# A hybrid encoder layer: a later rank for the residual, the second norm and the input factors of chunks 2 and 3

## The chip, the cores and the metric

One core of a Trainium2 chip runs the whole layer in one launch. The metric is device time in microseconds (us), lower is better. The kernel before was timed three times: 2137.07 us in the median, 2134.32 to 2137.93.

## The reference

The layer is a mixer (an S5 state space, a Fourier mixer and windowed attention side by side), an output projection with a residual, and a gated feed-forward network with a width-3 convolution. What matters here is the seam between the two:

```python
        y = jnp.concatenate([y_ssm.astype(x.dtype), y_fft.astype(x.dtype), y_att.astype(x.dtype)], axis=-1) @ w_out[l]
        x = x + gt_m * rms_norm(y, g_post_mix[l])

        h = rms_norm(x, g_pre_ffn[l]) * (1.0 + sc_f) + sh_f
        up = dwconv3(h @ w_up[l], conv_w[l], conv_b[l])
        gate, val = jnp.split(up, 2, axis=-1)
        y = (jax.nn.gelu(gate) * val) @ w_down[l]
        x = x + gt_f * rms_norm(y, g_post_ffn[l])
```

D_MODEL is 1024, SEQ 2048, D_FF 2816, all in float32. x is (1, 2048, 1024).

## The kernel before

Everything is held transposed: channels on the 128 partitions, positions along the free axis. The 2048 positions are cut into four chunks of 512 (c = 0 to 3). Float32 products are made from float16 halves: `mm3` issues three float16 matmuls (high by high, low by high, high by low) for one product.

**The seam.** `proj` (L1412) multiplies each chunk with the output weights, eight row blocks m = 0 to 7, 24 matmuls each. `proj_evac` copies a block out of its bank and adds its squares to a running sum. Then `post` (L1474) does, per chunk: the first norm, the residual (a multiply and an add per quarter of the channels, and a store of the result), the squares of it, the second norm, and the scale and shift for the feed-forward network. Each norm goes through `rnorm` (L344): one matmul with a matrix of ones sums the squares over the partitions, ACT takes a reciprocal root and squares it, and two DVE instructions refine it. The matmul writes a bank of the kind "m", of which there is one (`PTAGS`, L205), so a norm's matmul waits until the norm before it has been read out.

**The input factors.** `hcomb(p)` (L1562) turns the normalised chunks 2p and 2p+1 into seven sums and differences, each split into float16 halves. These feed a scheme of seven products for a 2 by 2 block product (`PLACE`). `hcomb(0)` serves positions 0 to 1023, `hcomb(1)` positions 1024 to 2047.

**The up-projection.** `ffn` (L1652) runs over p = 0, 1 and, in each, over 22 pairs of gate and value columns. A pair has seven products of 12 matmuls, in the order 1, 5, 6, 2, 7, 3, 4. Products 1, 6, 7 and 4 run up in the same bank (the pair's first), so each waits for the read of the one before: product 6 for an ACT copy of product 1, product 7 for an ACT copy of product 6, and product 4 for `up_add`, a DVE instruction that reads the bank after product 7. Product 5 opens a second bank that product 3 goes on in, product 2 has a third. `up_act` then does the convolution (four DVE instructions of 1023 elements, two on ACT), the gelu on ACT and the product with the value half. `wcomb` (L1545) makes the weight factors of a later pair, on DVE and ACT too; at most `W_LEAD` = 3 pairs ahead.

**What sets the order.** The program is recorded by coroutines. `Sched.run` picks the step that can start first by its own cost estimates, gives it a planned start st, and stamps the instructions with a rank (L191):

```python
            self.tc.cur_priority = 1000000 + int(PK * (st - p[4]))
```

PK is 100, p[4] is the third argument of `spawn` (`ahead`). A list scheduler then orders the instructions: on each engine the lowest rank first among those that its own estimates call ready. The result is one fixed sequence per engine (PE, DVE, ACT, POOL, and SP for the DMA issues). On the chip each engine takes its sequence from the top, and an instruction whose input is late holds those behind it.

Below, pair 0 to pair 6 are the first seven pairs of p = 0; their first banks are ps_5498, ps_7871, ps_8027, ps_8183, ps_8355, ps_8516 and ps_8662 in the rows of the order.

Of the kernel before, what the change touches and what calls it, by code (L numbers as in the profile page):

```python
# [43 lines left out]
S5_MUL = "V"  # L44
S5_ADD = "V"
G_M1 = 0
POST_B = 0.0
S5_B = 0.0
ATT_B = 0.0
X_AHEAD = (4, 4)  # L50
# [11 lines left out]
P_POST = 0  # L62
# [140 lines left out]
class Builder:  # L203
# [1208 lines left out]
    def proj(self):  # L1412
        self.x1d = self.dt([P, 8, T], F32)
        self.h2d = self.dt([7, 2, P, 2048], F16)
        for p in range(2):
            self.sc.spawn(self.hcomb(p), 0)
        q = [Fut() for _ in range(32)]
        lead = Sem(3)
        self.sc.spawn(self.wo_stream(q, lead))
        tail = Sem(TAIL)  # L1420
        for c in range(4):
            sl = slice(c * 512, (c + 1) * 512)
            tl = yield ("acq", tail, 1)
            yield ("w", self.f_gm)
            for f in self.f_ya[4 * c:4 * c + 4]:
                ta = yield ("w", f)
            yc = [self.u([2, 2, 512], F16) for _ in range(3)]
            fk = [Fut() for _ in range(5)]
            for k, f in enumerate(self.f_yssm + self.f_yfft):
                self.sc.spawn(self.yc_load(k, tl, f, yc[k // 2][:, k % 2], sl, fk[k]), 1)  # L1430
            ys = [self.u([2, 512]) for _ in range(4)]
            acc = self.u([2, 512])
            fs = [Fut() for _ in range(8)]
            for m in range(8):
                tw = yield ("w", q[8 * c + m])
                w = q[8 * c + m].val
                tb = yield ("acq", self.bank["z"], 1)
                ps = self.ps("z")
                t = max(tb, tw, tl, self.f_gm.t)
                for i, k in enumerate((5, 6, 7, 3, 4, 0, 1, 2)):  # L1440
                    if k < 5:
                        tk = yield ("w", fk[k])
                        r = yc[k // 2][:, k % 2, HI], yc[k // 2][:, k % 2, LO]
                    else:
                        tk = ta
                        r = self.yatt[c][HI][:, k - 5], self.yatt[c][LO][:, k - 5]
                    t = yield from self.mm3(max(t, tk), ps, (w[:, HI, k], w[:, LO, k]), r, i == 0, i == 7)
                lead.give(t)
                if 8 * c + m == self.ATT1:
                    self.f_pj.set(t)  # L1450
                if m == 7:
                    self.f_pc[c].set(t)
                self.sc.spawn(self.proj_evac(t, ps, ys[m // 2][:, m % 2], acc, m, fs))
            self.sc.spawn(self.post(c, fs, ys, acc, tail), P_POST if c else 0, 0.0 if c else POST_B)

    def yc_load(self, k, t, f, dst, sl, done):
        t1 = yield ("w", f)
# [652 lines left out]
```

## Time and profile before

| | |
|---|---|
| median of 3 runs (lowest, highest) | 2137.07 us (2134.32, 2137.93) |
| profiled execution, its own time | 2141.4 us |
| its span, first to last instruction | 2139.6 us |
| mean granted TensorE clock | 0.962 |
| PE busy | 1963.9 us, 92% of the span |
| DVE busy | 1559.8 us, 73% |
| ACT busy | 991.0 us, 46% |

Busy shares are means over stages with different limits. The mixer takes the first 840 us or so; chunks 2 and 3 pass the seam between about 860 and 1015 us, while the first pairs of the up-projection run; from there on the up-projection and the down-projection fill the rest. Times within the span are counted from its first instruction. L316 is the line of every matmul, L270 of every ACT instruction, L275 and L289 of DVE's two-input and three-input instructions, so the rows are told apart by shape: `u` is a work tile, `ps` a bank, `c` a constant.

### The profile page before, as it was taken

How to read it: one execution, taken by the hardware profiler on the slowest of the kernel's cores; microseconds unless marked ns; L12 is line 12 of the kernel's file. 1: busy time of each engine (PE TensorE's matmuls, PEld its weight loads, DVE VectorE, ACT ScalarE, POOL GpSimd, SP SyncE). 2: the span in 40 equal slices, each digit the busy share in tenths (PEclk: the TensorE clock that was granted, in tenths of full speed). 3: DMA queues.
4: the chain of work that ended last, by engine and by line, in shares of the span. 5: the costliest groups of instructions: out<-in, count | busy, mean ns of one | idle time of the engine just before them, and what ended most of it. 6: DMA issues, size and time to landing. Idle time of an engine off the chain costs nothing.

```text
span 2139.6 us, 26850 instructions
## 1 busy us (share of the span) xinstructions
PE 1963.9 (92%) x9796; PEld 967.3 (45%) x9796; DVE 1559.8 (73%) x2305; ACT 991.0 (46%) x1666; POOL 244.6 (11%) x310
## 2 busy tenths in 40 slices
PE   6788888789988889997999999999999999999997
PEld 1336764444543444443444444444444444434445
DVE  8998898869677767899988875666565763547356
ACT  3643333355566576665555543444444433322221
POOL 1566554002000000000000000000000000011002
PEclk9989999899999989998999999999999999999998
DMA  9362145673746333346655566656565494548533
GB/s 368 105 209 61 56 127 162 217 247 137 256 144 220 126 125 133 136 179 249 223 197 187 188 216 260 230 189 226 201 217 201 158 334 157 162 134 300 177 100 113
DMA packets 206663, 397.27 MB, mean 186 GB/s; under 512 B 19521, under 2 KB 111938, under 8 KB 206530
## 3 DMA queue, kind: packets, MB, share of 16 engines
q1 hardware_dynamic: 206530, 395.55, 53.7%
q8 instruction: 77, 1.26, 0.2%
q14 instruction: 56, 0.46, 0.1%
HBM read 258.93 MB, written 134.98 MB: 184 GB/s over the span
## 4 chain that ended last, share of the span: by engine, by line
PE 49%; DVE 8%; ACT 2%; issue 1%; DMA 1%; POOL 0%; SPq 0%; POOLq 0%; DVEq 0%; ACTq 0%
PE ps L316 49%; DVE u L289 4%; DVE u L275 3%; ACT u L270 2%; DMA u<-d 0%; DMA u<-w_up 0%; DMA d<-u 0%; ACT L270 0%; POOL u L275 0%; SPq L265 0%; POOLq L2095 0%; DVE u L282 0%; ACT c L270 0%; DVEq L289 0%; DVEq L275 0%
## 5 line engine op out<-in xcount | busy, mean ns | idle before, releaser
L316 PE MATMUL ps<-u,u 128*128 128x512 f16 (+5 forms) x9030 | 1879.2, 368 | 90.7 <-DVE u L289 40.5
L316 PEld LDWEIGHTS <-u 128*128 128x128 f16 (+1 forms) x9058 | 846.8, 99 | 1035.4 <-issue 157.6
L275 DVE TENSOR_TENSOR u<-u,u 128x512 f32<-128x512 f32 (+10 forms) x584 | 506.6, 900 | 105.9 <-ACT u L270 92.4
L270 ACT ACTIVATE u<-u 128x1024 f16<-128x1024 f32 (+7 forms) x485 | 406.0, 869 | 360.9 <-DVE u L275 150.3
L270 ACT ACTIVATE u<-ps 128x512 f32<-128x512 f32 (+8 forms) x497 | 268.7, 555 | 410.4 <-PE ps L316 377.5
L289 DVE SCALAR_TENSOR_TENSOR u<-u,c,u 128x1023 f32<-128x1023 f32 (+5 forms) x248 | 291.3, 1197 | 61.2 <-ACT u L270 53.9
L289 DVE SCALAR_TENSOR_TENSOR u<-ps,u 128x512 f32<-128x512 f32 (+4 forms) x231 | 152.3, 666 | 229.2 <-PE ps L316 199.2
L289 DVE SCALAR_TENSOR_TENSOR u<-u,u 128x1024 f16<-128x1024 f32 (+6 forms) x225 | 240.6, 1093 | 61.4 <-ACT u L270 58.1
L275 POOL TENSOR_TENSOR u<-u,u 128x288 f32<-128x288 f32 (+9 forms) x169 | 187.4, 1123 | 609.3 <-DVE u L289 462.4
L270 ACT ACTIVATE u<-u,c 128x1023 f32<-128x1023 f32 (+3 forms) x106 | 123.5, 1166 | 142.5 <-DVE u L289 122.7
L305 POOL MEMSET u<- 128x1 f32 x88 | 8.6, 98 | 1118.0 <-DVE u L289 415.8
L270 ACT ACTIVATE u<-u,st 128x384 f32<-128x384 f32 (+3 forms) x192 | 107.5, 592 | 30.8 <-DVE st L282 17.3
L316 PEld LDWEIGHTS ps<-u,u 128*128 128x128 f32 (+1 forms) x532 | 91.1, 180 | 39.9 <-DVE u L275 16.8
L316 PE MATMUL ps<-u,c 128*128 128x512 f32 (+4 forms) x142 | 61.8, 551 | 43.5 <-DVE u L300 18.5
L316 PE MATMUL ps<-c,u 128*128 128x128 f16 (+1 forms) x568 | 59.6, 229 | 23.9 <-ACT u L270 18.5
L270 ACT ACTIVATE c<-u 128x2 f32<-128x2 f32 (+1 forms) x88 | 17.8, 202 | 132.3 <-DVE u L289 132.2
L275 DVE TENSOR_TENSOR u<-u 128x512 f32<-128x512 f32 (+8 forms) x136 | 67.8, 502 | 12.4 <-ACT u L270 11.6
L300 DVE TENSOR_TENSOR_SCAN u<-u,u 128x512 f32<-128x512 f32 (+1 forms) x60 | 68.6, 1152 | 0.5
L1330 DVE CUSTOM_DVE_ANT_0 u<-ps,u 128x384 f32<-128x384 f32 (+1 forms) x96 | 48.1, 536 | 23.8 <-PE ps L316 23.7
L289 DVE SCALAR_TENSOR_TENSOR u<-u,st,u 128x384 f16<-128x384 f32 (+1 forms) x96 | 54.6, 603 | 12.2 <-ACT u L270 12.0
L270 ACT ACTIVATE u<-u,c,c 128x512 f32<-128x512 f32 (+1 forms) x64 | 48.4, 804 | 22.3 <-DVE u L275 6.2
L316 PEld LDWEIGHTS ps<-u,c 128*128 128x128 f32 (+1 forms) x142 | 23.9, 190 | 72.6 <-issue 46.6
(52 smaller groups left out, 370.9 us busy)
## 6 DMA issues: line engine op xcount, KB each, us to landing
u<-d SPq DMA_DIRECT2D x226, 512.0 KB
d<-u SPq DMA_DIRECT2D x158, 512.0 KB
d<-u SPq DMA_DIRECT2D x111, 256.0 KB
u<-w_ada SPq DMA_DIRECT2D x48, 512.0 KB
u<-w_up SPq DMA_DIRECT2D x44, 512.0 KB
u<-d SPq DMA_DIRECT2D x66, 256.0 KB
u<-x SPq DMA_DIRECT2D x32, 512.0 KB
u<-d SPq DMA_DIRECT2D x24, 511.0 KB
```

The costliest lines, as they stand in the source:

```text
L270: self.S.activation(out, in_, func, **kw)
L275: (self.V if eng == "V" else self.G).tensor_tensor(out, a, b, op)
L289: self.V.scalar_tensor_tensor(out, a, s, b, op0, op1)
L300: self.V.tensor_tensor_scan(out, d0, d1, 0.0, ALU.mult, ALU.add)
L305: (self.V if eng == "V" else self.G).memset(out, v)
L316: self.PE.matmul(o, a, b, start=st, stop=sp, skip_group_check=chain)
L1330: V.tensor_tensor_reduce(out=s_, in0=o, in1=self.bias[h // 2][:, h % 2, bo:bo + nk * 128], op0=ALU.add, op1=ALU.max, scale=1.0, scalar=-3e ...
```

## The change

The constant `POST_B` becomes a tuple by chunk, and `hcomb` gets an argument. For chunks 2 and 3 and for `hcomb(1)`, `ahead` is -150, which adds 15000 to the rank of every instruction that these coroutines issue: a place 150 us later by the planner's clock. The plan itself, the instructions, the tiles and the banks stay the same.

```diff
-POST_B = 0.0
+LATER = (0.0, 0.0, -150.0, -150.0)
...
         for p in range(2):
-            self.sc.spawn(self.hcomb(p), 0)
+            self.sc.spawn(self.hcomb(p), 0, -150.0 * p)
...
-            self.sc.spawn(self.post(c, fs, ys, acc, tail), P_POST if c else 0, 0.0 if c else POST_B)
+            self.sc.spawn(self.post(c, fs, ys, acc, tail), P_POST if c else 0, LATER[c])
```

The sequences of PE, DVE, ACT and SP change between about 858 and 1080 us of the trace of before; POOL's stays. Three places matter below.

**PE, at the matmul of the second norm of chunk 2** (`ps_7758<-u_7373,c_67`, with `c_67` the matrix of ones; `ps_7752` is the last block of the projection of chunk 3, `ps_7813` the first norm of chunk 3, `ps_8100` product 2 of pair 2, `ps_7871` the first bank of pair 1). Before:

```order
L316 LDWEIGHTS u_7684
L316 MATMUL ps_7752<-u_7423,u_7684 128x512
L316 MATMUL ps_7758<-u_7373,c_67 128x512
L316 LDWEIGHTS u_7684
L316 MATMUL ps_7752<-u_7421,u_7684 128x512
```

After:

```order
L316 LDWEIGHTS u_5625
L316 MATMUL ps_8100<-u_7531,u_5625 128x512
L316 MATMUL ps_7758<-u_7373,c_67 128x512
L316 MATMUL ps_7813<-u_7428,c_67 128x512
L316 LDWEIGHTS u_5493
L316 MATMUL ps_7871<-u_7501,u_5493 128x512
```

It stood within the last projection block. Now 119 more matmuls stand ahead of it: the other 9 of that block, 38 of pair 0 (the rest of products 2 and 7, and products 3 and 4), and products 1, 5 and 2 of pair 1 and of pair 2, 36 each. The first norm of chunk 3 follows at once, in the same bank.

**DVE, at the reader of that norm** (`u_7757<-ps_7758`; `ps_7662`, `ps_5498` and `ps_7606` are pair 0's products 2, 7 and 3, `u_6650` to `u_6653` are chunk 2's four quarters, `u_7881` is pair 0's convolution, `ps_7939` pair 1's product 2). Before:

```order
L275 TENSOR_TENSOR u_7373<-u_7373 128x512
L275 TENSOR_TENSOR u_7428<-u_7428 128x512
L289 SCALAR_TENSOR_TENSOR u_7757<-ps_7758,u_7757 128x512
L289 SCALAR_TENSOR_TENSOR u_7757<-u_7757 128x512
L275 TENSOR_TENSOR u_6650<-u_6650,u_7757 128x1024
L275 TENSOR_TENSOR u_7428<-u_7428 128x512
L289 SCALAR_TENSOR_TENSOR u_5496<-ps_7662,u_5496 128x512
L275 TENSOR_TENSOR u_6651<-u_6651,u_7757 128x1024
L289 SCALAR_TENSOR_TENSOR u_5497<-ps_5498,u_5497 128x512
```

After:

```order
L275 TENSOR_TENSOR u_7428<-u_7428 128x512
L289 SCALAR_TENSOR_TENSOR u_5496<-ps_7662,u_5496 128x512
L289 SCALAR_TENSOR_TENSOR u_5497<-ps_5498,u_5497 128x512
L289 SCALAR_TENSOR_TENSOR u_5496<-ps_7606,u_5496 128x512
L289 SCALAR_TENSOR_TENSOR u_7757<-ps_7758,u_7757 128x512
L289 SCALAR_TENSOR_TENSOR u_7757<-u_7757 128x512
L275 TENSOR_TENSOR u_6650<-u_6650,u_7757 128x1024
L275 TENSOR_TENSOR u_6651<-u_6651,u_7757 128x1024
L275 TENSOR_TENSOR u_6652<-u_6652,u_7757 128x1024
L275 TENSOR_TENSOR u_6653<-u_6653,u_7757 128x1024
L289 SCALAR_TENSOR_TENSOR u_7881<-u_5496,c_1115,u_7881 128x1023
L289 SCALAR_TENSOR_TENSOR u_7869<-ps_7939,u_7869 128x512
```

The reader moved back by four places only: the last sum of squares of chunk 3 and pair 0's three reads now stand ahead of it. All the rest of DVE's work, pair 0's convolution first, stands behind it in both.

**DVE, at the reads of pair 3** (`u_8182<-ps_8183` is the `up_add` that product 4 waits for; `u_8212`, `u_8213`, `u_8222`, `u_8286` and `u_8327` belong to `hcomb(1)`). Before:

```order
L275 TENSOR_TENSOR u_7424<-u_7426,u_7424 128x1024
L275 TENSOR_TENSOR u_8327<-u_8213,u_8326 128x1024
L275 TENSOR_TENSOR u_7425<-u_7427,u_7425 128x1024
L275 TENSOR_TENSOR u_8327<-u_8214,u_8326 128x1024
L289 SCALAR_TENSOR_TENSOR u_8181<-ps_8262,u_8181 128x512
L289 SCALAR_TENSOR_TENSOR u_8182<-ps_8183,u_8182 128x512
```

After:

```order
L289 SCALAR_TENSOR_TENSOR u_8193<-u_8193,u_8194 128x1023
L275 TENSOR_TENSOR u_8184<-u_8184,u_8186 128x512
L289 SCALAR_TENSOR_TENSOR u_8181<-ps_8262,u_8181 128x512
L275 TENSOR_TENSOR u_8222<-u_6651,u_8221 128x1024
L289 SCALAR_TENSOR_TENSOR u_8182<-ps_8183,u_8182 128x512
L275 TENSOR_TENSOR u_8213<-u_7426,u_8211 128x1024
```

The reads come ahead of much of `hcomb(1)`: ten fewer instructions stand ahead of this `up_add`. From the read `u_8661<-ps_8662` of pair 6 (its `up_add` before product 4) on, and already some 30 rows ahead of it, DVE has the same rows behind it in both sequences.

## The prediction

> **What bounds the kernel now.** I read the slices first, then windows over the places where the order changes, then the waits and the chain in them. The slices have 53.5 us each; number 17 covers about 856 to 909, number 20 about 1016 to 1070.
>
> ```profile
> PE   6788888789988889997999999999999999999997
> DVE  8998898869677767899988875666565763547356
> PEclk9989999899999989998999999999999999999998
> ```
>
> PE is full from slice 20 to the end, DVE around slices 18 to 20. The windows say it finer: per row the length, then busy time (and instructions) of each engine, and the granted clock.
>
> ```profile
> 892.00:1005.00 113.00, 98.05 (x431) 42.98 (x430) 108.70 (x116) 73.36 (x101) 1.08 (x11) 0.94 0.49 188
> 1005.00:1068.00 63.00, 60.59 (x280) 27.08 (x278) 59.28 (x66) 37.65 (x56) 0.79 (x8) 1.00 0.64 233
> 1068.00:1200.00 132.00, 132.00 (x613) 59.86 (x612) 107.85 (x116) 72.71 (x104) 1.47 (x15) 1.00 0.53 194
> 1200.00:1700.00 500.00, 500.00 (x2319) 226.68 (x2317) 324.53 (x340) 221.08 (x337) 5.01 (x51) 1.00 0.60 209
> ```
>
> Columns three and four are PE's weight loads and DVE. From 892 to 1068 DVE is busy for 167.98 of 176 us and PE for 158.64: DVE carries the work. From 1068 PE works 132.00 of 132 and DVE has 24 us to spare. So up to 1068 the end moves with DVE's sequence. Behind it PE has no gap in which lateness could run off. What PE lost before 1068:
>
> ```profile
> PE ps L316 <- DVE u L289: 15.1, 5, 10.7
> PE ps L316 <- ACT u L270: 2.1, 5, 0.7
> DVE u L289 <- ACT u L270: 10.3, 7, 3.5
> DVE u L289 <- DMA d<-u: 1.5, 1, 1.5
> ```
>
> These are waits between 860 and 1070: total, times, longest. PE waited 17.2 us, 10.7 of it once, on an `up_add`. The chain of waits shows what that one stood behind, and that nothing stops PE later:
>
> ```profile
> 966.00 2.96 DVE u L275 x3
> 968.96 4.01 DVE u L289 x4
> 972.97 4.54 DVE u L275 x4
> 977.51 1.21 DVE u L289 x2
> 978.77 5.29 PE ps L316 x12
> ...
> 1067.76 432.26 PE ps L316 x2002
> ```
>
> DVE worked without a break through `hcomb(1)`, then read the bank, then PE went on.
>
> **Part one: the `up_add` of pair 3 comes earlier.** Ten instructions fewer stand ahead of it, so the wait of 10.70 us should shrink or go. The rows that follow are PE's alone: start, length up to the next wait, instructions, and the wait ahead of them.
>
> ```profile
> 978.77 21.27 PE L316 MATMUL ps<-u,u 128*128 128x512 f16 x84 [10.70 <-DVE u L289]
> 1001.88 10.10 PE L316 MATMUL ps<-u,u 128*128 128x512 f16 x46 [1.84 <-DVE u L289]
> 1035.52 31.04 PE L316 MATMUL ps<-u,u 128*128 128x512 f16 x142 [0.82 <-DVE u L289]
> 1067.76 7.50 PE L316 MATMUL ps<-u,u 128*128 128x512 f16 x34 [1.21 <-DVE u L289]
> ```
>
> But work that DVE does later isn't done away with. The last two waits stand where DVE's sequence meets PE's again, after all that was put off: if DVE gets there no sooner, PE doesn't, and the gain is only PE's waits in another place. So I go by the time at which DVE gets there.
>
> **Part two: the matmul of chunk 2's second norm comes later on PE.** This decides the sum.
>
> ```profile
> 889.43 1.02 PE L316 MATMUL ps<-u,c 128*128 128x512 f32 x2
> ...
> 891.78 0.69 DVE L289 SCALAR_TENSOR_TENSOR u<-ps,u 128x512 f32<-128x512 f32 x1 [3.49 <-ACT u L270]
> ...
> 1034.78 1.28 DVE L289 SCALAR_TENSOR_TENSOR u<-ps,u 128x512 f32<-128x512 f32 x2
> ```
>
> Before, the matmul starts at 889.43, two ACT instructions follow, and DVE reads the bank at 891.78: 2.35 us later. After, 119 more matmuls stand ahead of it on PE. One takes 132.00/613 = 0.2153 us at the full clock, so they take 25.6 us and the matmul starts at 889.43 + 25.6 = 915.05. Their operands, the factors of positions 0 to 1023 and the first weights, were all written by 868.5 in the trace of before, so I add no wait; any wait would make it later still.
>
> DVE's reader moved back by only four places. Two reads in a row (the last row) take 1.28 us with 0.69 for the second, so a place costs 0.60 and the four 2.4 us. The last of the four reads product 3 of pair 0, which is done 35 of the 119 matmuls on, at 889.43 + 7.5 = 897; so DVE's turn comes at about 898. The bank is ready at 915.05 + 2.35 = 917.4. For some 19 us **DVE has nothing it may do**, with a full sequence behind the reader, in the stage that DVE carries: the rest of chunk 2's norm, pair 0's convolution, every read that PE waits for. PE meanwhile runs ahead until its banks are full and then waits for these reads.
>
> From there DVE's remaining work decides when it meets PE:
>
> ```profile
> 891.70:1035.50 143.80, 127.73 (x567) 56.14 (x565) 138.95 (x149) 91.94 (x129) 1.48 (x15) 0.95 0.54 202
> ```
>
> From that reader to the `up_add` of pair 6, DVE was busy for 138.95 us. After, the same rows are left but the four, 138.95 − 2.4 = 136.5. Without one gap DVE is through at 917.4 + 136.5 = 1053.9, where before PE went on at 1035.52: 18.4 later. By then PE has done 19 matmuls that stood behind this place before, 19 × 0.2153 = 4.1 us, so the end is late by 14.3. The wait of 1.21 at 1067.76 falls away, as PE is no longer ahead of DVE there: **+13.1 us is the low end**.
>
> To it come DVE's gaps. Before, it had 143.80 − 138.95 = 4.85 us of them in this stretch, nearly all waits for ACT (10.3 us from 860 on in the row above, some of it before 891.7). After, ACT starts from the same late norm, and the order of its work for chunk 3's norm, the scale and the bank copies gives the same sort of waits; stepping through the sequences by the trace's durations I get about 4.5. Ends: none (+13.1) and twice as many (+22.1); I take 4.5, as nearest to the row. **13.1 + 4.5 = +17.6 us.**
>
> **What I cost at nothing.** The stores of the residual and the factors of chunks 2 and 3 move behind loads and stores of weights on SP's queue. The weights then go out no later than before against their users, and the stored factors are needed for p = 1 only, hundreds of us on. The only wait on a transfer in the rows above is 1.5 us for a store: ends −1.5 and +1.5, I take 0. Were the cover gone and a weight load late, PE would stop for it in that stage, where it waits for DVE anyway. POOL's sequence stays and it has 1 us of work in 113. ACT is busy for 73.36 of 113: its moved instructions cost through DVE's gaps alone, counted already. The first norm of chunk 3 shares the bank and now follows at once, so PE should stop there about 2 us until DVE has read; PE has slack there.
>
> **PE's clock.** After the wait of 10.70 us, twelve matmuls take 5.29 us in the chain; twelve at 0.2153 are 2.6, so such a restart costs 2.7, and the granted clock is 0.94 from 892 to 1005. The hand timetable that gave the 4.5 has two long stops of PE after the change (about 6 us near 920, about 12 near 971), for the one of before. If they are hidden, since DVE is what comes last, they cost nothing; if the matmuls are on DVE's way, up to 2 × 2.7 = 5.4 more. The Trainium skill ("TensorE: Matmul & The Clock Gate", in "What's actually happening") has PE at half clock after an idle window of about 3.4 us, until it has been busy for one. The trace agrees: half speed for some 5 us after 10.70, none after 1.84. By that rule both stops are followed by a slow start, which speaks against this change, and the sum would be +23.0 instead of +17.6 if neither were hidden.
>
> **The rivals.**
>
> *The slow restarts reach DVE.* Each late product is read by DVE, so a slow one can open a gap there. For it: 10.70 us of idling did halve the speed. Against it: DVE is behind PE by up to a pair's reads there, with other work between. 17.6 + 5.4 = +23.0, 2160.1.
>
> *Faster: DVE doesn't run dry.* If the norm's matmul is ready before DVE's turn, only the savings stay: 10.70 + 1.84 + 0.82 + 1.21 of waits and the 2.7 of the restart, 17.3 us at most, 2119.8. It turns at one place: whether DVE has work until the bank is ready. For it: at the point in question DVE is the fuller engine. Against it: the order has the reader four rows, 2.4 us, later and the matmul 25.6 us later.
>
> *No change.* Lateness runs off before 1068, since PE had 17.2 us of waits there which the later norm may just fill. Against it: DVE's gaps from 891.7 to 1035.5 were 4.85 us in all, and lateness of DVE can run off only there. 2137.
>
> **How the numbers follow.** The profiled execution took 2141.4 us by its own time, with 2139.6 from first to last instruction; the median of the runs is 2137.07, 4.3 lower. The sum is a difference inside the trace: about 2159.0 for a profile, and I put it on the median: 2137.07 + 17.6 = **2154.7**. Chances: the forecast 0.74, the slow restarts 0.12, faster 0.08, no change 0.06. A measurement can tell about 0.2%, 4.3 us, from no change: slower by more than that 0.86, within 0.06, faster 0.08. The low end of the sum is 2150.2; the runs before are spread over 3.6 us, so the range starts 3 lower, at 2147. Above it takes in the twofold gaps (+22.1) and the slow restarts (+23.0), 2160, and ends 2 higher, at 2162. The two cases of the other signs, 0.14, stay outside.
>
> **What would show it.** Right: in the changed profile DVE idles for 15 to 20 us up to about 917, at a read of a bank (L289, released by ACT or PE); the norm's matmul stands near 915; PE's 10.70 wait is gone but has waits of the same sum between 916 and 985; PE is unbroken from about 1060 to 1085 on, everything behind it 15 to 20 us later. Wrong: DVE without a gap at 900 to 915 (then the faster rival holds), or PE with waits beyond 1100 that before doesn't have (then something else is late, weights first), or DVE's busy share from 917 to 1054 far below 0.97 (then ACT's place is mis-sized).

## The result and the profile after

The changed kernel takes 2160.38 us in the median of four runs (2158.64 to 2160.71), beside 2135.86 for the kernel before: 24.5 us more, a ratio of 1.0108 with a 95% interval of 1.0095 to 1.0122, or 20.3 to 26.1 us. Timed a second time beside other kernels it took 2158.92 against 2137.41: 21.5 us more, ratio 1.0095 (1.0081 to 1.0109). The profiled execution has a span of 2158.9 us and its own time is 2160.71.

The slices (54 us each here) show where it went. Slice 17 begins at about 864 us.

```profile
PE   6788888789988799977999999999999999999997
DVE  8998898869677667499998884656565664547356
PEclk9999998899999899988999999999999999999998
```

DVE has a 4 in slice 17 where it had an 8, and PE a 7 in slice 18 where it had a 9. The windows of the changed kernel, with the same columns as before (length, then PE, weight loads, DVE, ACT, POOL, clock, DMA):

```profile
892.00:1005.00 113.00, 88.17 (x367) 37.41 (x365) 84.21 (x89) 60.82 (x84) 0.59 (x6) 0.88 0.34 126
1005.00:1068.00 63.00, 56.42 (x255) 24.63 (x254) 61.26 (x66) 37.95 (x54) 0.98 (x10) 1.00 0.73 271
1068.00:1200.00 132.00, 130.52 (x604) 58.99 (x603) 112.33 (x124) 72.52 (x108) 1.38 (x14) 1.00 0.56 206
1200.00:1700.00 500.00, 500.00 (x2319) 226.68 (x2317) 326.83 (x342) 223.21 (x338) 5.30 (x54) 1.00 0.60 211
```

DVE is busy for 84.21 us of the first 113, and was for 108.70. Most of the loss arises in one smaller window. The kernel before:

```profile
898.00:917.00 19.00, 18.32 (x85) 8.22 (x84) 18.96 (x22) 16.00 (x22) 0.20 (x2) 1.00 0.24 91
```

The changed one:

```profile
898.00:917.00 19.00, 18.23 (x83) 8.03 (x81) 0.00 (x0) 1.50 (x4) 0.00 (x0) 1.00 0.00 1
```

In the same 19 us PE does as much as before. DVE does nothing at all, and ACT, POOL and the DMA next to nothing. The timeline of the changed kernel (start, length, engine, instruction, and in brackets the wait ahead of it) names what they wait for:

```profile
899.87 0.60 ACT L270 ACTIVATE u<-ps 128x512 f32<-128x512 f32 x1 [1.66 <-PE ps L316]
...
915.21 1.02 PE L316 MATMUL ps<-u,c 128*128 128x512 f32 x2
916.27 0.60 ACT L270 ACTIVATE u<-ps 128x512 f32<-128x512 f32 x1 [15.80 <-PE ps L316]
...
917.55 0.69 DVE L289 SCALAR_TENSOR_TENSOR u<-ps,u 128x512 f32<-128x512 f32 x1 [19.58 <-ACT u L270]
...
918.30 1.12 PE L316 MATMUL ps<-u,c 128*128 128x512 f32 x2 [2.07 <-DVE u L289]
```

The norm's matmul starts at 915.21 on PE, behind the products of pairs 0 to 2. ACT stands at the root of its result for 15.80 us, DVE at the read of its bank for 19.58. What PE then waits for, PE's rows alone:

```profile
925.86 13.06 PE L316 MATMUL ps<-u,u 128*128 128x512 f16 x48 [6.43 <-ACT u L270]
...
983.42 0.61 PE L316 MATMUL ps<-u,u 128*128 128x512 f16 x1 [10.25 <-ACT u L270]
984.87 20.14 PE L316 MATMUL ps<-u,u 128*128 128x512 f16 x83 [0.84 <-DVE u L289]
...
1059.54 22.68 PE L316 MATMUL ps<-u,u 128*128 128x512 f16 x103 [0.39 <-DVE u L289]
1082.97 40.18 PE L316 MATMUL ps<-u,u 128*128 128x512 f16 x185 [0.76 <-ACT u L270]
1123.88 601.04 PE L316 MATMUL ps<-u,u 128*128 128x512 f16 x2784 [0.72 <-DVE u L289]
1729.21 0.94 PE L316 MATMUL ps<-u,u 128*128 128x512 f16 x3 [4.30 <-ACT u L270]
```

The row at 1059.54 is product 4 of pair 6 (1035.52 before), the one at 1729.21 is the wait that stood at 1708.70 before. There PE is 20.5 us late, and nothing behind it has another order.

### The profile page after: what moved, and what is told of

Same layout as the page of the kernel before. It is cut to its first block, busy times and chain, and to the rows that moved or that the text cites. A ratio compares the mean times of both kernels' runs of the same rounds, so it can differ in the third digit from the quotient of the medians.

```text
span 2158.9 us, 26856 instructions
## 1 busy us (share of the span) xinstructions
PE 1969.2 (91%) x9796; PEld 968.6 (45%) x9796; DVE 1560.2 (72%) x2305; ACT 989.9 (46%) x1666; POOL 240.6 (11%) x310
## 4 chain that ended last, share of the span: by engine, by line
PE 51%; DVE 6%; ACT 2%; issue 2%; DMA 1%; POOL 0%; SPq 0%; POOLq 0%; DVEq 0%; ACTq 0%
PE ps L316 51%; DVE u L289 4%; ACT u L270 2%; DVE u L275 2%; DMA u<-d 0%; DMA u<-w_up 0%; POOL u L275 0%; ACT L270 0%; SPq L265 0%; POOLq L2095 0%; ACT c L270 0%; DVEq L289 0%; DVEq L275 0%; ACTq L270 0%
## 5 line engine op out<-in xcount | busy, mean ns | idle before, releaser
L270 ACT ACTIVATE c<-u 128x2 f32<-128x2 f32 (+1 forms) x88 | 17.9, 203 | 136.5 <-DVE u L289 136.3
```

The costliest lines, as they stand in the source:

```text
L270: self.S.activation(out, in_, func, **kw)
```

## The experiments

Two theories stood against each other. The first: the matmul of a norm goes back on PE much further than its reader goes back on DVE, and DVE and ACT, which take their instructions in order, run dry. The second: the mass of the put-off work (residual, scale and shift, input factors) is what comes too late. Each run was timed beside the kernel before; differences are of medians, in brackets by the 95% interval of the ratio.

### Half of the change: the input factors, or the chunks

```diff
-LATER = (0.0, 0.0, -150.0, -150.0)
+LATER = (0.0, 0.0, 0.0, 0.0)
```

> Only the input factors of positions 1024 to 2047 get the later rank; both chunks' residual and norms keep theirs. The norm's matmul of chunk 2 and its reader stand where they stood before, the read of pair 3 stands 11 places earlier on DVE, the one of pair 6 at its old place. Theory (the late norm's matmul leaves DVE without work): no idle DVE near 900 to 917, and DVE's place at pair 6 unchanged, so 0 less what PE has done ahead, 3 to 5 us faster than before. Rival (the late input factors and the stops they bring to PE are the loss): 5 to 15 us slower than before. Second rival (PE's waits by themselves are what counts): 13 to 17 us faster, as the 10.70 wait and its slow restart go.

2131.04 against 2136.55: 5.5 us faster (3.2 to 7.9), ratio 0.9974.

```diff
-            self.sc.spawn(self.hcomb(p), 0, -150.0 * p)
+            self.sc.spawn(self.hcomb(p), 0)
```

> Residual and second norm of chunks 2 and 3 late, input factors not. The norm's matmul stands 119 matmuls later, its reader 4 places later, and from the read of pair 3 on DVE's order is that of before. Theory: all of the loss is here, DVE idle about 19 us up to 917, no credit for matmuls done ahead at pair 6: 20 to 24 us slower than before. Rival (late input factors are the loss): within 5 us of before.

2161.77 against 2136.55: 25.2 us slower (22.2 to 28.6), ratio 1.0119, a little above the 20 to 24 us that were expected. DVE is idle for 19.59 us up to 916.70. The loss lies in the chunks' half; the input factors' half is a gain, also a little above its 3 to 5 us. The second theory falls here already, as far as it speaks of the input factors.

### The norm apart from the rest

For these, a coroutine can change its rank on the way (three lines in `_advance`, so line numbers are 3 higher: L319 for matmuls, L292, L278, L273). First everything behind the second norm late, and the norms early (`LATER` and the rank of `hcomb` as in the change):

```diff
+            if r[0] == "rank":
+                p[4], val = r[1], None
+                continue
...
-            self.sc.spawn(self.post(c, fs, ys, acc, tail), P_POST if c else 0, LATER[c])
+            self.sc.spawn(self.post(c, fs, ys, acc, tail), P_POST if c else 0, 0.0)
...
         tr = yield from self.rnorm(sqs, 512, rt[:, 0], rt[:, 1], slack)
         fq = []
+        yield ("rank", LATER[c])
```

> As the change, but chunks 2 and 3 take the later rank only behind the second norm (the products with its result, scale and shift, and the input factors). The matmul of chunk 2's second norm and its reader stand where they stood before. Theory: no idle DVE near 900 to 917; 3 to 5 us faster than before, so 23 to 29 us faster than the change. Rival (work put off behind the norm is the loss): 10 to 24 us slower than before.

2130.26 against 2136.55: 6.3 us faster (3.4 to 8.8), ratio 0.9971, a little above the 3 to 5 us expected, and some 29 us faster than the change. Then the opposite, against the kernel before and with the same three lines in `_advance`: everything at its old rank, and chunk 2's second norm alone late:

```diff
-POST_B = 0.0
+LATER = (0.0, 0.0, -150.0, 0.0)
...
-            self.sc.spawn(self.post(c, fs, ys, acc, tail), P_POST if c else 0, 0.0 if c else POST_B)
+            self.sc.spawn(self.post(c, fs, ys, acc, tail), P_POST if c else 0, 0.0)
...
+        yield ("rank", LATER[c])
         tr = yield from self.rnorm(sqs, 512, rt[:, 0], rt[:, 1], slack)
+        yield ("rank", 0.0)
```

> The order of before, but the second norm of chunk 2 alone (one matmul, two ACT and two DVE instructions) has the later rank; all else keeps its own. Its matmul stands 119 matmuls later, its reader 4 places later. Theory: these five instructions bring the whole loss, 20 to 24 us slower than before, DVE idle about 19 us up to 917. Rival (the mass of the put-off work is the loss): within 5 us of before.

2159.56 against 2136.55: 23.0 us slower (19.9 to 27.3), ratio 1.0111. In its timeline, DVE's row first and then PE's:

```profile
913.48 0.69 DVE L292 SCALAR_TENSOR_TENSOR u<-ps,u 128x512 f32<-128x512 f32 x1 [19.59 <-ACT u L273]
```

```profile
911.13 1.02 PE L319 MATMUL ps<-u,c 128*128 128x512 f32 x2
...
1087.91 636.65 PE L319 MATMUL ps<-u,u 128*128 128x512 f16 x2949 [1.20 <-DVE u L292]
1728.86 1.44 PE L319 MATMUL ps<-u,u 128*128 128x512 f16 x3 [4.29 <-ACT u L273]
```

One norm, five instructions, brings the whole loss, with the same idle time as in the change. The rest of what the change puts off costs nothing; in the version before this one it brings 6 us. Beside the late norm it brings something too: from the norm's matmul, which stands behind the same 119 others in both, to the wait near 1709 it is 1728.86 - 911.13 = 817.7 us here and 1729.21 - 915.21 = 814.0 in the change. These 3.7 us are about the 4.1 us of matmuls done ahead that the prediction counted; between the medians (23.0 us slower here, 24.5 and 21.5 for the change) they are lost in the spread. Windows of the version with the norms early, and two of PE's rows:

```profile
892.00:1005.00 113.00, 103.92 (x470) 45.80 (x468) 112.02 (x118) 78.61 (x107) 1.09 (x11) 1.00 0.53 196
1005.00:1068.00 63.00, 61.23 (x281) 27.18 (x279) 58.14 (x65) 36.91 (x55) 0.89 (x9) 1.00 0.63 233
```

```profile
1052.31 40.18 PE L319 MATMUL ps<-u,u 128*128 128x512 f16 x185 [0.75 <-ACT u L273]
1093.20 601.04 PE L319 MATMUL ps<-u,u 128*128 128x512 f16 x2784 [0.72 <-DVE u L292]
```

DVE fills 112.02 of 113 us (108.70 before) and PE does 39 matmuls more (470 against 431). PE's longest wait up to 1100 is 2.25 us and the clock stays at 1.00. So a wait of 10.70 us and a slow restart of 2.7 are gone, and the end moves by 6.3: part comes back as short waits (PE waits 11.2 us in all between 860 and 1100, where it waited 17.2), since DVE has the same work to do.

### The distance, and another norm

The change with -20 in place of -150, which puts the norm's matmul 71 places later instead of 119:

```diff
-LATER = (0.0, 0.0, -150.0, -150.0)
+LATER = (0.0, 0.0, -20.0, -20.0)
...
-        t = yield from self.ts(t, a, x, -150.0, 89.0, ALU.max, ALU.min)
+        t = yield from self.ts(t, a, x, -20.0, 89.0, ALU.max, ALU.min)
...
-            self.sc.spawn(self.hcomb(p), 0, -150.0 * p)
+            self.sc.spawn(self.hcomb(p), 0, -20.0 * p)
```

The line in the middle isn't part of the idea: the edit also reached a -150 that is the lower bound of a clamp in an exponential (`exp48`). It changes a number that one instruction takes, not the order or the shapes, and the reading below rests on a wait at the seam itself.

> The change with -20 in place of -150. The matmul of chunk 2's second norm stands 71 matmuls later than before instead of 119, its reader 4 places later as in the change; the reads of pairs 3 and 6 stand where the change has them. Theory (loss goes with the matmuls ahead of the norm's): bank ready 48 x 0.2153 = 10.3 us earlier than in the change, DVE idle about 9 us instead of 19.6, so 9 to 12 us faster than the change. Rival (the put-off work on DVE behind the reader is the loss): within 4 us of the change, as those places are the same.

2146.16 against 2137.41: 8.7 us slower (5.8 to 13.3), ratio 1.0045, and 12.8 faster than the change timed beside it (2158.92). The end of the expected range was 12. One of its six runs took 2156.49, the other five 2143.54 to 2146.39. Its DVE:

```profile
902.38 0.69 DVE L289 SCALAR_TENSOR_TENSOR u<-ps,u 128x512 f32<-128x512 f32 x1 [9.23 <-ACT u L270]
```

9.23 us instead of 19.58, for 48 matmuls fewer (10.3 us). The loss goes with the number of matmuls. Then chunk 3 and the input factors late, chunk 2 as before:

```diff
-LATER = (0.0, 0.0, -150.0, -150.0)
+LATER = (0.0, 0.0, 0.0, -150.0)
```

> Chunk 3 and the input factors late, chunk 2 as before. Chunk 2's second norm stands as before; chunk 3's first norm stands 96 matmuls later (20.7 us, so near 916), its reader 4 places later on DVE. Theory (any norm whose matmul goes back on PE further than its reader on DVE): DVE idle about 15 us at that reader, 9 to 15 us slower than before. Rival (only chunk 2's second norm matters): 3 to 6 us faster than before, like the run with the input factors alone.

2152.01 against 2137.41: 14.6 us slower (11.3 to 17.1), ratio 1.0066. The time is as expected; the place isn't.

```profile
913.69 0.60 ACT L270 ACTIVATE u<-ps 128x512 f32<-128x512 f32 x1 [14.96 <-PE ps L316]
914.19 1.23 ACT L270 ACTIVATE u<-u,c 128x1023 f32<-128x1023 f32 x1
...
915.51 1.28 DVE L289 SCALAR_TENSOR_TENSOR u<-u,c,u 128x1023 f32<-128x1023 f32 x1 [18.59 <-ACT u L270]
```

DVE doesn't stop at the norm's reader but ahead of it, at pair 0's convolution: its first part is an ACT instruction (914.19) that stands behind the root of the late norm (913.69) on ACT. So the queue of ACT alone is enough to hold DVE, and a reader further back on DVE would not have helped.

### The change and the kernel before, once more

> The change itself again, beside the other kernels. The trace of the change shows PE 20.5 us later from 1709 on and a span 19.3 us longer than the one trace of before; the medians were 23 to 24.5 apart. Theory: the trace of before was a long execution of it (2141.4 against a median near 2136.5), so 22 to 25 us slower than before by the medians. Rival: 18 to 20 us.

21.5 us slower (17.3 to 23.3), just below the expected 22 to 25 and above the rival's 18 to 20; the interval doesn't tell them apart. Its trace has the same rows as the first: DVE idle for 19.59 us, waits of PE of 6.43 and 9.23.

> The kernel before, traced again. Eight other traces have 427.7 to 429.7 us from the start of PE at about 1709 to 1733 to the end of the span, where no sequence differs; the one trace of before has 430.9. Theory (the first trace of before was long in its tail and in nothing of the change): the same waits of PE at the seam (about 10.7, 1.8, 0.8, 1.2 us) and a tail of 427.5 to 430. Rival (something in the change shortens the tail): a tail of about 430.9 again.

One run, 2137.02, with a span of 2135.2. PE's rows:

```profile
977.23 8.31 PE L316 MATMUL ps<-u,u 128*128 128x512 f16 x27 [10.69 <-DVE u L289]
...
1066.00 636.65 PE L316 MATMUL ps<-u,u 128*128 128x512 f16 x2949 [1.20 <-DVE u L289]
1706.94 1.44 PE L316 MATMUL ps<-u,u 128*128 128x512 f16 x3 [4.29 <-ACT u L270]
```

The waits at the seam are those of the first trace to 0.01 us. The tail from 1706.94 is 2135.2 - 1706.94 = 428.3 us, where the first trace has 2139.6 - 1708.70 = 430.9. So the trace that the prediction stands on was 2.6 us long in the tail and 1.8 up to that wait, and the 19.3 us between the two first spans is too small: from this trace to the first one of the change it is 2158.9 - 2135.2 = 23.7, to the second (2157.2) 22.0.

### Towards a faster version

From the version with the norms early: the eight sums of `hcomb(1)` on POOL, which is almost idle there.

```diff
-        e = H_ADD
+        e = "G" if p else H_ADD
```

> The version with the norms early and the rest late, and the eight sums of the second pair of chunks' input factors on POOL instead of DVE (8 x 1.14 us of DVE, 8 x 2.66 of POOL). Theory (DVE's work up to about 1050 sets the end): DVE gets to pair 6 some 9 us earlier, up to 9 us faster than the version without, 2121 to 2128. Rival (waits for POOL stand in DVE's sequence, or PE's waits for ACT now come last): within 3 us of it or slower.

2140.75 against 2137.41: 3.3 us slower than before (1.5 to 6.0), some 10 slower than the version without. The window from 892 and a piece of the timeline:

```profile
892.00:1005.00 113.00, 96.57 (x424) 42.00 (x422) 112.34 (x103) 70.71 (x99) 26.38 (x17) 0.94 0.45 168
```

```profile
956.17 1.21 DVE L292 SCALAR_TENSOR_TENSOR u<-u,u 128x1024 f16<-128x1024 f32 x1
956.78 11.74 POOL L278 TENSOR_TENSOR u<-u,u 128x1024 f32<-128x1024 f32 x4 [2.67 <-issue]
957.31 2.84 DVE L278 TENSOR_TENSOR u<-u 128x512 f32<-128x512 f32 x1
960.08 3.42 DVE L292 SCALAR_TENSOR_TENSOR u<-u,c,u 128x1023 f32<-128x1023 f32 x1
963.42 5.65 DVE L278 TENSOR_TENSOR u<-u,u 128x512 f32<-128x512 f32 x2
```

DVE is as busy as without (112.34 to 112.02 us) but does 103 instructions instead of 118. Beside POOL's sums an addition that takes 0.69 elsewhere takes 2.84, and two of them 5.65: about as long as one of POOL's sums each (11.74/4 = 2.9). So the theory failed, and the time is the rival's ("or slower") without its reasons: no wait for a result of POOL stands between 860 and 1080, DVE runs slower beside POOL. PE's long wait for DVE is back, 10.59 us at 974.39. The Trainium skill ("SBUF — State Buffer", in "SBUF: two separate sides") has DVE, with two inputs in SBUF, and the GpSimd engine share a pair of ports that one of them holds for a whole instruction. The trace agrees: from 957.31 four DVE instructions take 11.8 us beside four sums of POOL in 11.74, one each in turn.

The bank reads first, again from the version with the norms early:

```diff
-                self.sc.spawn(self.up_add(t, b1, U[1][:, n1], f[5], f[7], False))
+                self.sc.spawn(self.up_add(t, b1, U[1][:, n1], f[5], f[7], False), 0, 40.0)
```

(and the same for the other two `up_add`.)

> The version with the norms early and the rest late, and the bank reads of the up-projection on DVE with a rank 40 us earlier. The read of pair 6 stands 4 places earlier than there, but 13 matmuls fewer are done ahead of it (2.8 us); that of pair 8 stands at the same place. Theory (DVE's amount of work up to pairs 6 to 8 sets the end, not which of it comes first): within 3 us of that version, 2127 to 2133. Rival (PE's waits for these reads set it): 5 us or more faster, below 2126.

2128.66 against 2137.32: 8.7 us faster than before (4.9 to 10.9), ratio 0.9963; 1.6 from the version without, within the expected 3. This and the version with the norms early beat both kernels; which of them is the better one these runs don't tell.

## Why the prediction was right

The forecast was 2154.7, 17.6 us slower, in a range of 2147 to 2162. Measured: 2160.38 and 2158.92, inside it, and 20.5 us in the trace. By the number alone the rival with the slow restarts (2160.1) is nearer to the medians than the forecast; that its number fits is luck, as its mechanism isn't in the trace (the point on PE's clock below).

- **The late matmul.** 915.05 forecast, 915.21 found; the bank read at 917.4, found at 917.55. DVE idle about 19 us from 898: 19.58.
- **DVE's remaining work.** 136.5 us forecast from that reader to the read of pair 6. The window of the changed kernel has 136.60:

```profile
917.55:1059.50 141.95, 112.02 (x472) 47.61 (x473) 136.60 (x145) 89.87 (x122) 1.37 (x14) 0.90 0.54 199
```

- **DVE's gaps** were sized at 4.5 and are 141.95 - 136.60 = 5.35. With the 0.15 of the reader and the 0.1 of the work, product 4 of pair 6 starts at 1059.54 and not at 1058.4: 1.1 us of what is missing.
- **The step that failed: "the wait of 1.21 at 1067.76 falls away".** In its place PE waits 0.76 for ACT at 1082.97 and 0.72 for DVE at 1123.88, 1.48 us together. From product 4 of pair 6 to the wait near 1709, with the 4.1 us of matmuls done ahead taken off, the lateness goes from 24.02 - 4.1 = 19.9 to 20.5, instead of down by 1.2. That is the other 1.8 us: 17.6 + 1.1 + 1.8 = 20.5. The reason given, that PE is no longer ahead of DVE there, was wrong: the two still meet until 1123.88, and PE is unbroken only from there to the wait near 1729, not from 1060 to 1085. The new order sets these waits, not the lateness: the version with the norms early, which is faster than before, has both (0.75 and 0.72), and the one with the norm alone late keeps the old one (1.20). A wait beyond 1100 was the prediction's own sign that something else is late, weights first. No transfer stands in the chain of waits of the changed kernel from 1055 to 1123.88; it runs over DVE and ACT.
- **A sign that didn't hold.** PE was to have "waits of the same sum" as the 10.70 between 916 and 985. They come to 24.8 us, which cost no more than said above because DVE is behind PE there.
- **The earlier read of pair 3.** The prediction said that a wait saved on PE is no gain while DVE gets there no sooner. The runs with the late input factors alone and with the norms early bear it out: 5.5 and 6.3 us, not the 17.3 of the rival in which DVE doesn't run dry.
- **PE's stops and its clock.** Forecast were stops of about 6 and 12 us; found 6.43 and 10.25. After them 48 matmuls take 13.06 us and 83 take 20.14, where at 0.2153 they would take 10.3 and 17.9: restarts of 2.7 and 2.3 us. They were hidden, as the forecast had it and the rival didn't: from the reader to the read of pair 6, DVE waits for PE only once, for 0.50 us (at 994.11), while PE goes on waiting for ACT and DVE. A slow matmul could still reach DVE by way of ACT, but all of DVE's gaps together are 5.35 us, 0.5 more than before. The Trainium skill ("TensorE: Matmul & The Clock Gate", in "What's actually happening") has PE at half clock after an idle window of about 3.4 us. The trace agrees, after the wait of 6.43 us too; here this sets PE's pace and not the end.
- **The stores and loads on SP, taken at nothing.** The run with one norm alone late leaves them at their old rank and loses as much as the change, so they had no part in it that can be told.
- **From the trace to the median.** The sum was put on the median of before. The two medians are 21.5 and 24.5 apart, the trace gives 20.5; both intervals contain it. Where the remaining 1 to 4 us come from isn't shown. The runs of the kernel before spread from 2131 to 2142, and a part of that lies ahead of the seam: the matmul of chunk 2's second norm starts at 889.43 in the first trace of before, at 888.38 in the second and at 886.35 with only the input factors late, and PE's order up to it is the same in all three.

## What to carry to other kernels

A later rank on a whole coroutine moves each of its instructions past whatever stands in the sequence of its own engine: one norm's matmul went back 25 us on PE and its reader 2 us on DVE, and DVE and ACT, which take their work in order, stood idle for the time in between. When work is put off, keep the links that cross engines (matmul, root, read) at their old rank and put off what others don't wait for soon, as the version with the norms early does. A long wait on an engine that isn't the full one is worth little: 13 us of it were taken away here for 6.

## What the runs showed of the hardware

An engine that looks free isn't free of charge: POOL's additions of 128x1024, put beside a full DVE, stretched DVE's additions from 0.69 to 2.84 us, and the move lost some 10 us where up to 9 were expected as a gain.
